# Gate matrix build of a two-layer diffusion trunk: dense selection masks, evacuations on ACT, one gated group in four on GpSimd, more one-hot buffers

## The chip, the cores and the metric

One NeuronCore of a Trainium2 chip runs the whole kernel. The metric is the device time of one execution in microseconds; the median of three runs counts. The engines are TensorE (PE; its weight loads are PEld), VectorE (DVE), ScalarE (ACT), GpSimd (POOL) and SyncE (SP), which only issues DMAs here.

## The reference, cut to what matters

Two layers of a trunk over 640 tokens (128 context, 512 latent). Each layer mixes tokens (gated linear attention, a short convolution, neighbourhood attention) and then retrieves single-neuron experts:

```python
s1 = jnp.einsum('thd,hnd->thn', q[..., :half], k1)      # 8 heads, 128 keys each
s2 = jnp.einsum('thd,hnd->thn', q[..., half:], k2)
v1, i1 = lax.top_k(s1, 16)
v2, i2 = lax.top_k(s2, 16)
cand = v1[..., :, None] + v2[..., None, :]              # 256 candidates a head
cidx = i1[..., :, None] * 128 + i2[..., None, :]
top, pos = lax.top_k(cand, 16)
idx = take_along_axis(cidx, pos); g = softmax(top)      # 128 experts a token
act = gelu(einsum('td,thkd->thk', x, u[idx]))
out = einsum('thk,thkd->td', g * act, v[idx])
```

There are 16384 experts a layer, as 128 rows of 128 columns; expert = 128 * i1 + i2.

## The kernel before

Tokens 0 to 255 take their experts by indirect DMA (`gather`, L736 to L759, issued by POOL). Tokens 256 to 639 are done densely: all 16384 experts are computed in 128 blocks, and each result is multiplied by a gate that is zero for experts that were not chosen. The gates of a token are a 128 x 128 matrix (row of the expert, column of the expert) with 128 nonzero places, one for each choice.

**select(t)** turns the two top-16 lists of 128 tokens into lists of chosen experts, all on DVE but for one exponential. A position in the ordered list of 50 candidates is compared with 16 thresholds (`mask`, L694), the 0/1 mask is multiplied with the differences of the index list (`lookup`, L688), and the 16 products are added by halving (`fold`, L683 and L685). This is done three times: for the first index, for the offset of the row, for the second index. The mask tile is laid out [choice, threshold], with the 16 thresholds last; its two operands are the positions, repeated along the last axis, and the thresholds, repeated along the middle one.

**build(tcn)** makes the gate matrices of 16 tokens. For eight tokens at a time DVE writes two one-hot tiles by comparison with a counter: `ohp` (L776, f32, the expert's row) and `ohq` (L778, bf16, the column). For four tokens at a time ACT multiplies the columns by the gate of each choice, one token an instruction (L782, `qg`), PE multiplies `qg` and `ohp` of each token into PSUM (L785), and the result is evacuated in two parts: the first two groups of rows stay resident in SBUF (`gres`, L787, ACT), the other 14 go to `sg` and from there to DRAM (L795). The spilled part of the first of the four groups of a build is copied by DVE (L791), of the other three by ACT (L793). There are two buffers each of `ohp` and `ohq` and three of `qg`; PSUM has four for these products.

**Order.** After the first top-k stage, peer() runs select(2), then by `ORDER` the builds of tokens 256 to 383 (b2), select(3), b3, select(4), the first top-k of tokens 0 to 127 (l1(0), L610 to L618), b4, select(0). The tile framework lays out each engine's instructions in one fixed order, and independent steps are mixed in it: selects and l1 stand between the builds on DVE. In layer 0, each build also takes a step of the adaLN projection of layer 1 (`next(ada)`, L794: PE, ACT and DVE work and 1 MB of weights). The gate stage, here, is the stretch from the first one-hot tile to the last evacuation: 24 builds a layer.

**After it** come the 128 dense blocks (`dense`): each loads 1 MB, splits it on ACT and DVE (L829, L830), and multiplies on PE; two gathers go with each block.

Of the kernel before, what the change touches and what calls it, by code (L numbers as in the profile page):

```python
# [10 lines left out]
F32 = mybir.dt.float32  # L11
# [4 lines left out]
BF16 = mybir.dt.bfloat16  # L16
F16 = mybir.dt.float16
AF = mybir.ActivationFunctionType
OP = mybir.AluOpType
# [9 lines left out]
PH = 8  # L29
# [29 lines left out]
BSEL = 16  # L59
EVD = 1  # L60
NQG = 3
GLAG = 1
# [3 lines left out]
class Trunk:  # L66
    def __init__(self, ctx, tc, I, O):
# [3 lines left out]
        V, S = self.V, self.S  # L71
        pers = ctx.enter_context(tc.tile_pool(name="pers", bufs=1))
        consts = pers
# [10 lines left out]
        self.ident = const("ident", [128, 128])  # L84
        self.nstep = consts.tile([128, 16], F16, name="nstep16")
        self.thr = consts.tile([128, 2, 16], F16, name="thr16")
        self.iota = consts.tile([128, 128], BF16, name="iota16")
# [4 lines left out]
        with tc.tile_pool(name="init", bufs=1) as ip:  # L92
            for name, shape, dst, dt in (("cT", [128, 8, 2], None, F32), ("lmask", [128, 7, 128], self.lmask, I32),
                                         ("thr", [128, 2, 16], self.thr, F32), ("nstep", [128, 16], self.nstep, F32),
                                         ("iota", [128, 128], self.iota, F32)):
                t = ip.tile(shape, dt, name="i_" + name)
                nc.scalar.dma_start(t, I[name])
                if dst is None:
                    S.activation(self.sc[:, :, 0:2], t, AF.Silu)
                else:  # L100
                    V.tensor_copy(dst, t)
# [463 lines left out]
    def peer(self, l):  # L565
        tc, nc, I = self.tc, self.nc, self.I
        V, S, G, PE = self.V, self.S, self.G, self.PE
# [11 lines left out]
        i12 = [None] * 5  # L579
# [53 lines left out]
        def select(t):  # L633
# [30 lines left out]
            g = gg[t] if t < 2 else ks.tile([128, 128], F32, name="g", tag="g")  # L664
            gv = g.rearrange("p (h k) -> p h k", h=PH)
            V.tensor_tensor(gv, top, top[:, :, 0:1].to_broadcast([128, PH, 16]), op=OP.subtract)
# [3 lines left out]
            V.reciprocal(gz, gz)  # L670
            V.tensor_tensor(gv, gv, gz[:, :, None].to_broadcast([128, PH, 16]), op=OP.mult)
            dl = ks.tile([128, 2, PH, 16], F16, name="dl", tag="dl")
            V.tensor_copy(dl[:, :, :, 0:1], i12[t][:, :, :, 0:1])
            V.tensor_tensor(dl[:, :, :, 1:], i12[t][:, :, :, 1:], i12[t][:, :, :, :15], op=OP.subtract)
            pf = ks.tile([128, 128], F16, name="pf", tag="pf")
            V.tensor_copy(pf, pos.rearrange("p h k -> p (h k)"))
            sh = [128, 128, 16]
            mk = ks.tile(sh, F16, name="mk", tag="mk")
            m2 = ks.tile(sh, F16, name="m2", tag="m2")

            def fold(out, src):
                for w in (8, 4, 2):
                    V.tensor_tensor(m2[:, :, :w], src[:, :, :w], src[:, :, w:2 * w], op=OP.add)  # L683
                    src = m2
                V.tensor_tensor(out, m2[:, :, 0], m2[:, :, 1], op=OP.add)  # L685

            def lookup(out, a):
                V.tensor_tensor(m2.rearrange("p (h k) m -> p h k m", h=PH),  # L688
                                mk.rearrange("p (h k) m -> p h k m", h=PH),
                                dl[:, a, :, None, :].to_broadcast([128, PH, 16, 16]), op=OP.mult)  # L690
                fold(out, m2)

            def mask(a):
                V.tensor_tensor(mk, pf[:, :, None].to_broadcast(sh), self.thr[:, a, None, :].to_broadcast(sh), op=OP.is_ge)  # L694

            ij = ks.tile([128, 3, 128], F16, name="ij", tag="ij")
            mask(0)
            lookup(ij[:, 0], 0)
            V.tensor_tensor(m2, mk, self.nstep[:, None, :].to_broadcast(sh), op=OP.mult)
            fold(ij[:, 2], m2)  # L700
            V.tensor_tensor(pf, pf, ij[:, 2], op=OP.subtract)
            mask(1)
            lookup(ij[:, 1], 1)
            f3 = ks.tile([128, 2, 128], F32, name="f3", tag="f3")
# [65 lines left out]
        def build(tcn):  # L770
            sg = bp.tile([128, NSP, GB, TC], F32, name="sg", tag="sg")
            for t8 in range(0, TC, 8):
                t0 = tcn * TC + t8
                ohp = bp.tile([128, 8, 128], F32, name="ohp", tag="ohp")
                ohq = bp.tile([128, 128, 8], BF16, name="ohq", tag="ohq")
                V.tensor_tensor(ohp, ixT[:, 0, t0:t0 + 8, None].to_broadcast([128, 8, 128]),  # L776
                                self.iota[:, None, :].to_broadcast([128, 8, 128]), op=OP.is_equal)
                V.tensor_tensor(ohq, ixT[:, 1, None, t0:t0 + 8].to_broadcast([128, 128, 8]), iota8, op=OP.is_equal)  # L778
                for t4 in range(0, 8, 4):
                    qg = bp.tile([128, 4, 128], F32, name="qg", tag="qg", bufs=NQG)  # L780
                    for t in range(4):
                        S.activation(qg[:, t, :], ohq[:, :, t4 + t], AF.Copy, scale=gT[:, t0 + t4 + t:t0 + t4 + t + 1])  # L782
                    ps = pss.tile([128, 4, 128], F32, name="ps_g", tag="s")
# [5 lines left out]
                    so, sp = sg[:, :, :, tt:tt + 4].rearrange("p r b t -> p (r b) t"), ps[:, :, NR * GB:].rearrange("p t b -> p b t")  # L789
                    if (tt // 4) % 4 < EVD:  # L790
                        V.tensor_copy(so, sp)  # L791
                    else:
                        S.activation(so, sp, AF.Copy)  # L793
            next(ada, None)  # L794
# [206 lines left out]
```

## Time and profile before

| what | value |
|---|---|
| median of three runs (lowest, highest) | 4094.76 us (4085.15, 4112.63) |
| the profiled execution | 4098.88 us, its span 4097.1 us |
| busy in the span | PE 92%, DVE 81%, ACT 42%, POOL 18% |
| mean granted clock of PE | 0.951 of 2.4 GHz |
| bytes over the DMA queues | 1011.79 MB, mean 247 GB/s |

A profile describes one execution. "Busy" is time in which an engine has an instruction under way; PE's ends are modelled. Instructions of one engine overlap a little in the profile, so the distance between two starts is a better price than the duration of one. A line such as L785 is a line of the kernel.

### The profile page before, as it was taken

What the parts mean: (1) busy time and instruction counts of PE and PEld (TensorE: products, weight loads), DVE (VectorE), ACT (ScalarE), POOL (GpSimd) and SP (SyncE); (2) the same over time, 40 slices, a digit from 0 to 9 for tenths busy, and PEclk for the clock granted to TensorE, in tenths of its full rate; (3) what the DMA queues carried; (4) which work ended last, traced back from release to release, by engine and by line L of the source; (5) the groups of instructions that cost most, each with busy time, mean ns of one, the idle gap of its engine ahead of it and who ended that gap; (6) DMA issues with size and microseconds to landing.
All of it is one profiled execution on the core that took longest, in us unless ns stands there. A gap on an engine that the chain in (4) does not pass through costs nothing.

```text
span 4097.1 us, 52986 instructions
## 1 busy us (share of the span) xinstructions
PE 3752.5 (92%) x19892; PEld 3210.2 (78%) x19892; DVE 3324.4 (81%) x6613; ACT 1701.8 (42%) x3269; POOL 755.8 (18%) x532
## 2 busy tenths in 40 slices
PE   7999996888999999999989999867799999999998
PEld 5897875557888888888879988745688888888886
DVE  3863478778999999999968533988899999999997
ACT  4423334883333333333354242378633333333333
POOL 0000000003333333333300000000133333333331
PEclk8999997878999999999999999978799999999999
DMA  5114142648999999999911121022699999999995
GB/s 178 33 61 139 65 144 80 190 133 345 381 378 388 382 382 383 391 379 386 364 53 34 61 65 52 32 72 90 226 366 377 382 383 385 379 386 382 380 379 211
DMA packets 263089, 1011.79 MB, mean 247 GB/s; under 512 B 21872, under 2 KB 110320, under 8 KB 164272
## 3 DMA queue, kind: packets, MB, share of 16 engines
q0 software_dynamic: 73728, 536.90, 34.0%
q1 hardware_dynamic: 171392, 425.43, 27.8%
q10 hardware_dynamic: 17712, 46.07, 2.9%
q8 instruction: 157, 2.57, 0.2%
q14 instruction: 100, 0.82, 0.1%
HBM read 960.49 MB, written 47.84 MB: 246 GB/s over the span
## 4 chain that ended last, share of the span: by engine, by line
issue 34%; PE 34%; POOL 11%; DVE 8%; ACT 8%; DMA 5%; POOLq 0%; ACTq 0%; DVEq 0%; SPq 0%
PE ps_pj L225 13%; POOL uv L745 11%; DMA uv<-uv,gidx 4%; ACT qg L782 4%; PE ps_g L785 4%; PE acc L868 3%; PE ps_lv L353 2%; PE ps_ada L150 2%; PE npo L519 1%; ACT sg L793 1%; PE ps_ms L167 1%; PE ps_s L498 1%; PE ps_a L852 1%; PE ps_a L851 1%; PE ps_a L850 1%
## 5 line engine op out<-in xcount | busy, mean ns | idle before, releaser
L745 POOL DMA_INDIRECT uv<-uv,gidx x512 | 748.5, 1462 | 3272.0 <-DVE gacc L757 1354.2
L850 PE MATMUL ps_a<-hd,uhi 128*128 128x384 f32 x2048 | 693.9, 339 | 33.8 <-ACT uhi L829 33.8
L852 PE MATMUL ps_a<-hd,ulo 128*128 128x384 f32 x2048 | 693.3, 339 | 10.0 <-DVE ulo L830 10.0
L851 PE MATMUL ps_a<-hd,uhi 128*128 128x384 f32 x2048 | 692.0, 338 | 0.0
L748 DVE SCALAR_TENSOR_TENSOR uv<-uv,ht 128x1024 f32<-128x1024 f32 x512 | 622.5, 1219 | 84.0 <-DMA uv<-uv,gidx 83.0
L757 DVE SCALAR_TENSOR_TENSOR gacc<-uv,gw,gacc 128x1024 f32<-128x1024 f32 x508 | 652.1, 1284 | 15.5
L868 PE MATMUL acc<-vhi,whi 128*128 128x512 f32 x1536 | 504.3, 410 | 33.9 <-ACT whi L860 33.3
L868 PE MATMUL acc<-vhi,wlo 128*128 128x512 f32 x1536 | 483.0, 396 | 15.8 <-DVE wlo L861 15.7
L829 ACT ACTIVATE vhi<-raw 128x1024 fp32r<-128x1024 f32 x256 | 272.2, 1063 | 537.6 <-PE acc L868 523.1
L868 PE MATMUL acc<-vlo,whi 128*128 128x512 f32 x1536 | 477.5, 392 | 0.0
L850 PEld LDWEIGHTS ps_a<-hd,uhi 128*128 128x128 f32 x2048 | 387.9, 189 | 46.5 <-ACT uhi L829 36.2
L785 PE MATMUL ps_g<-ohp,qg 128*128 128x128 f32 x1536 | 333.2, 359 | 83.5 <-ACT qg L782 82.2
L785 PEld LDWEIGHTS ps_g<-ohp,qg 128*128 128x128 f32 x1536 | 261.4, 235 | 184.4 <-ACT qg L782 142.6
L852 PEld LDWEIGHTS ps_a<-hd,ulo 128*128 128x128 f32 x2048 | 387.4, 189 | 16.6 <-DVE ulo L830 14.6
L851 PEld LDWEIGHTS ps_a<-hd,uhi 128*128 128x128 f32 x2048 | 387.9, 189 | 10.2
L868 PEld LDWEIGHTS acc<-vhi,whi 128*128 128x128 f32 x1536 | 270.0, 188 | 128.2 <-ACT whi L860 81.2
L782 ACT ACTIVATE qg<-ohq,gT 128x128 f32<-128x128 bf16 x768 | 339.6, 526 | 65.7 <-DVE ohq L778 65.7
L868 PEld LDWEIGHTS acc<-vhi,wlo 128*128 128x128 f32 x1536 | 282.8, 188 | 92.6 <-DVE wlo L861 34.4
L868 PEld LDWEIGHTS acc<-vlo,whi 128*128 128x128 f32 x1536 | 289.0, 188 | 65.0
L830 DVE TENSOR_TENSOR vlo<-raw,vhi 128x1024 fp32r<-128x1024 f32 x256 | 311.8, 1218 | 16.0 <-ACT vhi L829 15.9
L830 DVE TENSOR_TENSOR ulo<-raw,uhi 128x1024 fp32r<-128x1024 f32 x256 | 312.2, 1220 | 2.1 <-ACT uhi L829 2.0
L750 ACT ACTIVATE gw<-dots 128x2 f32<-128x2 f32 x256 | 52.0, 203 | 610.0 <-DVE uv L748 610.0
(242 smaller groups left out, 6085.6 us busy)
## 6 DMA issues: line engine op xcount, KB each, us to landing
raw<-dn SPq DMA_DIRECT2D x256, 1024.0 KB
wada<-w_ada SPq DMA_DIRECT2D x48, 1024.0 KB
gsp<-sg SPq DMA_DIRECT2D x48, 896.0 KB
gres<-gsp ACTq DMA_DIRECT2D x112, 384.0 KB
wraw<-w_in SPq DMA_DIRECT2D x56, 512.0 KB
wraw<-w_out SPq DMA_DIRECT2D x16, 512.0 KB
wraw<-wq SPq DMA_DIRECT2D x16, 512.0 KB
uv<-uv,gidx POOLq DMA_INDIRECT x512
```

Of the source, the lines that this page charges most:

```text
L225: self.PE.matmul(ps[j][:, :n], w[:, k, :], x[:, k, :], start=(k == 0 and i == 0), stop=(k == 7 and i == 2))
L745: G.indirect_dma_start(out=b, out_offset=None, in_=I["uv"], in_offset=bass.IndirectOffsetOnAxis(ap=gidx[t][:, s:s + 1], axis=0))
L748: V.scalar_tensor_tensor(b[:, :D], b[:, :D], 1.0, ht[t], op0=OP.mult, op1=OP.mult, accum_out=dots[:, s:s + 1])
L757: V.scalar_tensor_tensor(acc_, b[:, D:], w[:, s:s + 1], acc_, op0=OP.mult, op1=OP.add)
L782: S.activation(qg[:, t, :], ohq[:, :, t4 + t], AF.Copy, scale=gT[:, t0 + t4 + t:t0 + t4 + t + 1])
L785: PE.matmul(ps[:, t, :], qg[:, t, :], ohp[:, t4 + t, :], start=True, stop=True)
L829: S.activation(hi, raw, AF.Copy)
L830: V.tensor_tensor(lo, raw, hi.bitcast(F32), op=OP.subtract)
L850: PE.matmul(ps, uhi[:, ks], hd[0][:, k, :], start=(k == 0), stop=False)
L851: PE.matmul(ps, uhi[:, ks], hd[1][:, k, :], start=False, stop=False)
L852: PE.matmul(ps, ulo[:, ks], hd[0][:, k, :], start=False, stop=(k == 7))
L868: PE.matmul(acc[:, t, j, :], a[:, ts], x[:, j * 512:(j + 1) * 512], start=(b == 0 and i == 0), stop=(b == 127 and i == len(parts) - 1))
```

## The change

Three things.

1. In `select` the mask, the differences, the positions and the constants are laid out with the head (8 of them) as the last axis, so that both operands of a mask have a dense last axis, and the folds run over the outer axis. The choices of a token are numbered by (choice, head) and no longer by (head, choice), in the gates too. The exponentials are written to the first 16 columns of the candidate tile.
2. In `build`, the gated rows of the last of four groups are made by one GpSimd product over four tokens; the other three stay on ACT. ACT evacuates the spilled part of all four groups.
3. Buffers: `qg` 5 for 3, `ohp` 3 for 2, `ohq` 4 for 2.

```diff
-EVD = 1
-NQG = 3
+NQG = 5
+QGP = (3,)
@@ constants
-        self.nstep = consts.tile([128, 16], F16, name="nstep16")
-        self.thr = consts.tile([128, 2, 16], F16, name="thr16")
+        self.nstep = consts.tile([128, 16, PH], F16, name="nstep16")
+        self.thr = consts.tile([128, 2, 16, PH], F16, name="thr16")
+                elif name in ("thr", "nstep"):
+                    V.tensor_copy(dst, t[..., None].to_broadcast(shape + [PH]))
@@ select
-            gv = g.rearrange("p (h k) -> p h k", h=PH)
+            gv = cand[:, :, :16]
...
-            V.tensor_tensor(gv, gv, gz[:, :, None].to_broadcast([128, PH, 16]), op=OP.mult)
-            dl = ks.tile([128, 2, PH, 16], F16, name="dl", tag="dl")
+            V.tensor_tensor(g.rearrange("p (k h) -> p h k", h=PH), gv, gz[:, :, None].to_broadcast([128, PH, 16]), op=OP.mult)
+            dl = ks.tile([128, 2, 16, PH], F16, name="dl", tag="dl")
...
-            pf = ks.tile([128, 128], F16, name="pf", tag="pf")
-            V.tensor_copy(pf, pos.rearrange("p h k -> p (h k)"))
-            sh = [128, 128, 16]
+            pf = ks.tile([128, 16, PH], F16, name="pf", tag="pf")
+            V.tensor_copy(pf, pos.rearrange("p h k -> p k h"))
+            sh = [128, 16, 16, PH]
...
-                    V.tensor_tensor(m2[:, :, :w], src[:, :, :w], src[:, :, w:2 * w], op=OP.add)
+                    V.tensor_tensor(m2[:, :w], src[:, :w], src[:, w:2 * w], op=OP.add)
                     src = m2
-                V.tensor_tensor(out, m2[:, :, 0], m2[:, :, 1], op=OP.add)
+                V.tensor_tensor(out.rearrange("p (k h) -> p k h", h=PH), m2[:, 0], m2[:, 1], op=OP.add)
+            def per(x):
+                return x[:, :, None, :].to_broadcast(sh)
...
-                V.tensor_tensor(mk, pf[:, :, None].to_broadcast(sh), self.thr[:, a, None, :].to_broadcast(sh), op=OP.is_ge)
+                V.tensor_tensor(mk, pf[:, None].to_broadcast(sh), per(self.thr[:, a]), op=OP.is_ge)
@@ build
-                ohp = bp.tile([128, 8, 128], F32, name="ohp", tag="ohp")
-                ohq = bp.tile([128, 128, 8], BF16, name="ohq", tag="ohq")
+                ohp = bp.tile([128, 8, 128], F32, name="ohp", tag="ohp", bufs=3)
+                ohq = bp.tile([128, 128, 8], BF16, name="ohq", tag="ohq", bufs=4)
...
-                    for t in range(4):
-                        S.activation(qg[:, t, :], ohq[:, :, t4 + t], AF.Copy, scale=gT[:, t0 + t4 + t:t0 + t4 + t + 1])
+                    if (t8 + t4) // 4 in QGP:
+                        G.tensor_tensor(qg.rearrange("p t q -> p q t"), ohq[:, :, t4:t4 + 4],
+                                        gT[:, None, t0 + t4:t0 + t4 + 4].to_broadcast([128, 128, 4]), op=OP.mult)
+                    else:
+                        for t in range(4):
+                            S.activation(qg[:, t, :], ohq[:, :, t4 + t], AF.Copy, scale=gT[:, t0 + t4 + t:t0 + t4 + t + 1])
...
-                    if (tt // 4) % 4 < EVD:
-                        V.tensor_copy(so, sp)
-                    else:
-                        S.activation(so, sp, AF.Copy)
+                    S.activation(so, sp, AF.Copy)
```

## Rows read from the trace of the kernel before

**Rows 1.** Windows, dense stretches: busy (count) of PE, PEld, DVE, ACT, POOL; PEclk, DMA, GB/s.

```profile
1000.00:1950.00 950.00, 922.83 (x4563) 812.23 (x4562) 896.02 (x1208) 340.46 (x542) 321.06 (x219) 1.00 0.97 383
3000.00:3950.00 950.00, 919.40 (x4530) 805.84 (x4528) 890.04 (x1200) 338.54 (x540) 317.66 (x217) 1.00 0.97 381
```

**Rows 2.** Windows: before layer 1's gate stage, the stage itself, layer 0's gate stage.

```profile
2648.00:2689.30 41.30, 9.04 (x36) 6.25 (x34) 41.30 (x244) 2.08 (x3) 0.00 (x0) 0.62 0.00 1
...
2689.30:2915.30 226.00, 177.27 (x782) 136.26 (x782) 187.59 (x560) 205.34 (x555) 2.09 (x3) 0.81 0.30 95
675.00:921.00 246.00, 211.50 (x1016) 143.46 (x1017) 186.51 (x545) 210.54 (x559) 0.20 (x1) 0.83 0.53 163
```

**Rows 3.** Chain that ended last, shares by line: layer 1's gate stage, then layer 0's.

```profile
by line: ACT qg L782 45.7%; PE ps_g L785 24.2%; ACT sg L793 12.5%; ACT gres L787 5.0%; issue 1.9%; DVE i L614 1.4%; DVE i L618 1.4%; DVE ohp L776 1.2%; POOL uv L745 1.1%; DVE v L616 1.0%; DVE s L612 0.9%; DVE ohq L778 0.9%; DVE v L610 0.7%;
by line: PE ps_g L785 37.6%; ACT qg L782 21.4%; PE ps_ada L150 18.2%; ACT sg L793 7.4%; ACT gres L787 3.3%; DMA uv<-uv,gidx 2.7%; PE ps_at L157 2.5%; DVE ohp L776 1.4%; issue 1.1%; DVE i L618 0.9%; DVE ohq L778 0.7%; DVE v L616 0.6%; DVE i 
```

**Rows 4.** Waits, layer 1's gate stage: waiter <- releaser: us in total, times, longest.

```profile
ACT qg L782 <- DVE ohq L778: 33.0, 3, 19.5
...
DVE ohq L778 <- ACT qg L782: 15.2, 29, 1.9
DVE sg L791 <- ACT gres L787: 13.6, 22, 1.1
DVE ohp L776 <- PE ps_g L785: 8.4, 17, 1.5
```

**Rows 5.** Timeline at the seam to b4: start, length, engine, line [idle before it].

```profile
2829.74 0.42 DVE L715 CAST ixT<-pt 128x256 bf16<-128x256 f32 x1 [0.88 <-PE pt L713]
...
2844.46 3.83 ACT L782 ACTIVATE qg<-ohq,gT 128x128 f32<-128x128 bf16 x9 [12.91 <-DVE ohq L778]
```

**Rows 6.** Timeline of ACT in layer 1's gate stage, steady state.

```profile
2766.43 0.54 ACT L793 ACTIVATE sg<-ps_g 128x448 f32<-128x448 f32 x1
2766.86 1.76 ACT L782 ACTIVATE qg<-ohq,gT 128x128 f32<-128x128 bf16 x4
2768.51 0.21 ACT L787 ACTIVATE gres<-ps_g 128x64 f32<-128x64 f32 x1
2768.61 0.54 ACT L793 ACTIVATE sg<-ps_g 128x448 f32<-128x448 f32 x1
```

**Rows 7.** DVE by line and shape (L791: layer 1's stage): count, busy us, mean ns, idle.

```profile
L778 DVE TENSOR_TENSOR ohq<-ixT,iota 128x1024 bf16<-128x1024 bf16 x96 | 66.1, 688 | 31.3 <-ACT qg L782 31.2
L694 DVE TENSOR_TENSOR mk<-pf,thr 128x2048 f16<-128x2048 f16 x20 | 45.7, 2285 | 0.1
L688 DVE TENSOR_TENSOR m<-mk,dl 128x2048 f16<-128x2048 f16 x20 | 24.4, 1219 | 0.0
L685 DVE TENSOR_TENSOR ij<-m 128x128 f16<-128x128 f16 x30 | 11.7, 390 | 0.1
L683 DVE TENSOR_TENSOR m<-m 128x256 f16<-128x256 f16 x30 | 11.7, 389 | 0.1
L701 DVE TENSOR_TENSOR pf<-pf,ij 128x128 f16<-128x128 f16 x10 | 2.2, 219 | 0.1
...
L791 DVE COPY sg<-ps_g 128x448 f32<-128x448 f32 x24 | 15.0, 624 | 13.6 <-ACT gres L787 13.6
```

**Rows 8.** POOL's memsets; then gather issues and L830: ns min/median/max, first and last start.

```profile
L281 POOL MEMSET qz<- 64x640 f32 x8 | 5.0, 627 | 14.6 <-DVE gacc L757 14.1 <-POOLq L992 0.3
L282 POOL MEMSET st<- 64x256 f32 x8 | 2.4, 304 | 0.0
...
L745 POOL DMA_INDIRECT uv<-uv,gidx x512: 933/1674/3284, 920.8 to 4041.7; - x171
...
L830 DVE TENSOR_TENSOR ulo<-raw,uhi x256: 1210/1220/1226, 933.5 to 4045.1; 128x1024 fp32r<-128x1024 f32 x128
L830 DVE TENSOR_TENSOR vlo<-raw,vhi x256: 1211/1218/1227, 941.6 to 4048.9; 128x1024 fp32r<-128x1024 f32 x128
```

**Rows 9.** Windows, L785 alone: PE and PEld busy (count), PEclk, DMA share, GB/s.

```profile
2724.00:2731.00 7.00, 5.59 (x27) 3.86 (x26) 1.00 0.42 131
2804.50:2812.50 8.00, 7.39 (x31) 6.64 (x30) 0.50 0.36 115
```

More of the change, by code (lines that the diff above doesn't have):

```diff
@@ L670, in select @@
             V.reciprocal(gz, gz)
-            V.tensor_tensor(gv, gv, gz[:, :, None].to_broadcast([128, PH, 16]), op=OP.mult)
-            dl = ks.tile([128, 2, PH, 16], F16, name="dl", tag="dl")
-            V.tensor_copy(dl[:, :, :, 0:1], i12[t][:, :, :, 0:1])
-            V.tensor_tensor(dl[:, :, :, 1:], i12[t][:, :, :, 1:], i12[t][:, :, :, :15], op=OP.subtract)
-            pf = ks.tile([128, 128], F16, name="pf", tag="pf")
-            V.tensor_copy(pf, pos.rearrange("p h k -> p (h k)"))
-            sh = [128, 128, 16]
+            V.tensor_tensor(g.rearrange("p (k h) -> p h k", h=PH), gv, gz[:, :, None].to_broadcast([128, PH, 16]), op=OP.mult)
+            dl = ks.tile([128, 2, 16, PH], F16, name="dl", tag="dl")
+            ix = i12[t].rearrange("p a h m -> p a m h")
+            V.tensor_copy(dl[:, :, 0:1, :], ix[:, :, 0:1, :])
+            V.tensor_tensor(dl[:, :, 1:, :], ix[:, :, 1:, :], ix[:, :, :15, :], op=OP.subtract)
+            pf = ks.tile([128, 16, PH], F16, name="pf", tag="pf")
+            V.tensor_copy(pf, pos.rearrange("p h k -> p k h"))
+            sh = [128, 16, 16, PH]
             mk = ks.tile(sh, F16, name="mk", tag="mk")
@@ L682, in fold, with lookup @@
                 for w in (8, 4, 2):
-                    V.tensor_tensor(m2[:, :, :w], src[:, :, :w], src[:, :, w:2 * w], op=OP.add)
+                    V.tensor_tensor(m2[:, :w], src[:, :w], src[:, w:2 * w], op=OP.add)
                     src = m2
-                V.tensor_tensor(out, m2[:, :, 0], m2[:, :, 1], op=OP.add)
[L687 to L690, printed above, removed]
+                V.tensor_tensor(out.rearrange("p (k h) -> p k h", h=PH), m2[:, 0], m2[:, 1], op=OP.add)
+            def per(x):
+                return x[:, :, None, :].to_broadcast(sh)
+            def lookup(out, x):
+                V.tensor_tensor(m2, mk, per(x), op=OP.mult)
                 fold(out, m2)
             def mask(a):
-                V.tensor_tensor(mk, pf[:, :, None].to_broadcast(sh), self.thr[:, a, None, :].to_broadcast(sh), op=OP.is_ge)
+                V.tensor_tensor(mk, pf[:, None].to_broadcast(sh), per(self.thr[:, a]), op=OP.is_ge)
             ij = ks.tile([128, 3, 128], F16, name="ij", tag="ij")
             mask(0)
[L698 to L701, printed above, removed]
+            lookup(ij[:, 0], dl[:, 0])
+            lookup(ij[:, 2], self.nstep)
+            V.tensor_tensor(pf, pf, ij[:, 2].rearrange("p (k h) -> p k h", h=PH), op=OP.subtract)
             mask(1)
-            lookup(ij[:, 1], 1)
+            lookup(ij[:, 1], dl[:, 1])
             f3 = ks.tile([128, 2, 128], F32, name="f3", tag="f3")
```

## The prediction

> **What bounds the kernel now.** I read the windows first, then the chain of waits inside the stretch that the change touches, then who waited there, then single durations. The two dense stretches, where all 128 expert blocks of a layer run, hold the DMA engines at 0.97 of their time and PE at 0.97 busy with the full clock granted [rows 1]. The change removes no byte and no matmul there, so nothing can be won in them. The work that is edited lies in the gate stage of each layer: 24 builds, 226.0 us in layer 1 and 246.0 us in layer 0, with the DMA engines at 0.30 and 0.53, plus the stretch before it in which select(2) runs alone and DVE is busy for 41.30 of 41.30 us [rows 2]. Whatever comes off these comes off the end one for one, since the dense stretch starts when the last build is out.
>
> In layer 1's gate stage ACT is busy 205.3 us, DVE 187.6, PE 177.3 [rows 2]. The chain agrees: 45.7 + 12.5 + 5.0 = 63.2% of it is ACT (gating the one-hot rows, then the two evacuations) and 24.2% PE. In layer 0 the adaLN matmuls of the next layer are mixed in, and the chain turns: PE has 37.6 + 18.2 + 2.5 = 58.3%, ACT 21.4 + 7.4 + 3.3 = 32.1% [rows 3]. So a gift to ACT is worth about half as much in layer 0. ACT's own waits are one start-up wait of 19.5 us, which began before the stage, and one of 12.9 us at the seam to the last eight builds [rows 4, 5]: there DVE finishes the index lists at 2829.74 but works through the rest of l1(0) before the next one-hot tile, and ACT starts again only at 2844.46.
>
> **ACT's part.** In steady state a gating quartet takes ACT from 2766.86 to 2768.51, 1.65 us; the resident part 0.10; the spilled part from 2766.43 to 2766.86, 0.43 [rows 6]. Per build the change takes one quartet of four from ACT and gives it the one spilled part that DVE copied: 1.65 - 0.43 = 1.22 us less. Over 24 builds that is 29.3 us, so ACT goes from 205.3 to 176.0 in layer 1.
>
> **DVE's part, without POOL.** The 24 copies of L791 leave: 15.0 us, and with them 13.6 us of waiting for ACT [rows 4, 7]. In every select, two masks of 2048 elements take 2.285 us, while the product on the same 2048 half-precision elements, whose last axis is dense, takes 1.219 [rows 7]. After the edit the masks' last axis is eight dense elements in both operands. That eight are enough I read from L778: a comparison too, last axis eight, 1024 elements in 0.688. So 2 x (2.285 - 1.219) = 2.13 us. The rows at 2048 (1.219) and 128 (0.219) elements make 0.52 ns an element and 0.15 fixed, which gives 0.29 for the dense fold of 256 in place of 0.389, and 0.219 for the last fold in place of 0.390 [rows 7]; three folds a select save 3 x 0.10 + 3 x 0.17 = 0.81. Together 2.9 us a select; the bound below is nothing (masks that stay at 2.285). Select(2) stands bare ahead of each stage: 2 x 2.9 = 5.9 us straight off the end. Three more selects run inside each stage: 8.8 us of DVE time. DVE in layer 1 goes to 187.6 - 15.0 - 8.8 = 163.8.
>
> **The product on POOL.** POOL is idle in the stage (2.1 us busy) [rows 2], so nothing stands ahead of the product in its queue. Behind it, PE's four matmuls of that group wait for it, then every later matmul in PE's order, then ACT's evacuations of that group. No row shows an elementwise operation of POOL. Its memsets take 0.627 us for 640 elements and 0.304 for 256 [rows 8]: 0.84 ns an element and 0.09 fixed. One pass over 512 elements would be 0.52 us, the floor. Two reads and one write, one after another, make 1.38. The same engine's gather issue takes 0.93 us at best and 1.67 in the median, when DVE is busy beside it, 1.8 times as much [rows 8]; that factor gives 2.5, and the longest gather, 3.28, is my upper end. I take 1.9, between 1.38 and 2.5. Even 3.28 is below the 7.3 us that ACT will need for a build (176.0 / 24), so POOL itself is not the bound.
>
> What it takes from DVE is the open price. Below: nothing, because L830, which reads two SBUF tensors, takes 1210 to 1227 ns in 512 instances, most of them in a stretch where POOL issues its gathers [rows 8]. Above: the whole product, since a gather issue hardly reads SBUF and the product reads two operands. I take 1.2 us, some two thirds of 1.9, because a part of DVE's work in the stage (the top-k searches) has one operand. The Trainium skill speaks against the change here: "SBUF — State Buffer", section "Who interferes with whom", says that a DVE instruction with two SBUF inputs and a GpSimd instruction that reads SBUF exclude each other for the whole instruction. By that rule the price is the full length of the product, which is the second rival below; the rows of L830 neither show nor exclude it. The Trainium skill's "GPSIMD Engine Reference", section 3.1, gives 4497 ns for a two-input operation on 2048 elements, which no run here shows; an estimate from that page is 1.1 us for 512, DVE's price at the same two thirds 0.7, and the sum 12 us shorter a layer.
>
> **Parts at nothing.** The one-hot and gated tiles take more buffers; that costs no instruction, and it takes away some of DVE's 15.2 and 8.4 us of waiting for ACT and PE [rows 4]. The permuted gate weights, index differences and positions have as many instructions as before. The exponentials now lie in the candidate tile, so the next select's candidates wait for one more small product. The two longer constant copies stand at the kernel's start beside the first loads; bare they would be under 1 us. Select(1) runs in the dense stretch, behind DMA [rows 1]. With POOL as idle as it is, the last product is out before the first gather may go.
>
> **PE's clock.** In the stretch 2724 to 2731 the full clock is granted and PE, paced by ACT, is busy 5.59 of 7.00 us; in 2804.5 to 2812.5 it is 1.2 GHz and PE is busy 7.39 of 8.00 [rows 9]. So a build at 1.2 GHz has little room left below today's pace; this caps the gain wherever the clock stays low, and I count it in layer 0.
>
> **The sum.** Layer 1: DVE 163.8 + 24 x 1.2 = 192.6, above ACT's 176.0. DVE sat idle for 226.0 - 187.6 = 38.4 us; 13.6 go with the copies and the deeper buffers take part of the rest, so I leave 12. That makes 204.6, 21 us less. Layer 0: ACT's relief by its share of the chain, 29.3 x 32.1 / 63.2 = 15 us. Select(2): 5.9. In all 42.2 us. The profiled execution took 4098.9 us (span 4097.1); 4098.9 - 42.2 = 4056.7. The median of the runs, 4094.8, is 4.1 lower, so I forecast 4053 for the median.
>
> **The rivals.**
> - DVE loses nothing to POOL and ACT stays the bound. For it: L830's even durations. Layer 1 gains the full 29.3, layer 0 perhaps 22, plus 5.9: 57 us, 4037. If the wait of 12.9 us at the seam goes too, in both layers, 4012.
> - The product shuts DVE out for its whole length of 1.9 us, or the masks stay at 2.285. For it: DVE will be close behind ACT. DVE is then 163.8 + 45.6 + 12 = 221, a gain of 5 a layer and 5.9: 4079. Without the masks' gain (5.9 in all and 8.8 in each layer lost) the forecast would be 4076. By the exclusion rule of the Trainium skill, named above, the first half of this is the case.
> - Slower: the product is long under DVE's traffic and shuts DVE out. The point that decides is a loss of (226.0 - 163.8 - 12) / 24 = 2.1 us a build. At 3.28, DVE has 163.8 + 78.7 + 12 = 254.5, 28.5 us more in each layer; less 5.9 that is 51 us, 4146. For it: four-element runs and a strided output, on an engine that no row shows at such work. Against it: it needs both the long product and the full exclusion.
>
> **How the numbers follow.** Measurement of this kernel tells about 1% from no change, so faster is below 4054, slower above 4136. Forecast (4040 to 4066): 0.38. First rival (4010 to 4040): 0.25. Second (4066 to 4100): 0.26. Slower side: 0.11, of which 0.09 beyond 1%. Faster is the first rival and two thirds of the forecast's band, 0.50; same 0.41; slower 0.09. The range 4015 to 4092 leaves out the slower side and the outermost of the first two. The forecast's own range is 4040 to 4066.
>
> **What would show it.** Right: L694 near 1.22 us; ACT in layer 1's stage near 176 us; the stage near 205; a POOL product near 1.9 us; L776 and L778 lengthened or held up beside it by about 1.2 us a build; the stretch before the stage 3 us shorter. Wrong: L776 even at 1.22 with no idle time (first rival); products above 2.5 us with DVE near 100% busy (second, third); a seam wait that grows as ACT runs ahead of DVE.

## The result and the profile after

The changed kernel takes 4027.59 us in the median (4024.19 to 4033.49), the kernel before, run beside it, 4101.16 us (4085.15 to 4112.63). The ratio is 0.9826, with a 95% interval from 0.9807 to 0.9844: 74 us less by the two medians, 71 by the ratio, where 42 were forecast. The profiled execution after took 4028.24 us (span 4026.5), against a span of 4097.1 before, so the two profiles differ by 70.6 us.

Where these 70.6 us went, read from the starts of four lines in both traces (first one-hot tile; last gate matmul; first transposition of the second gathered tile of tokens, some 8 us before that of the dense blocks' output; end):

| stretch | before | after | difference |
|---|---|---|---|
| up to layer 0's first one-hot tile | 675.0 | 675.3 | +0.3 |
| layer 0's gate stage | 247.9 | 199.6 | -48.3 |
| layer 0's dense stretch | 1136.9 | 1154.8 | +17.9 |
| up to layer 1's first one-hot tile | 629.6 | 622.9 | -6.7 |
| layer 1's gate stage | 225.0 | 191.6 | -33.4 |
| layer 1's dense stretch | 1143.7 | 1143.0 | -0.7 |
| the rest | 39.0 | 39.3 | +0.3 |

The gate stages gave 81.7 us, and the dense stretches, which the change does not touch, took back 17.2. These are two single executions; how far they repeat is said further down. Below, the "stage" is always the stretch of this table. The windows shown run 0.2 to 1.3 us past it, so where a microsecond matters, busy times are taken over the stage itself (DVE 175.5 and 176.2 us in the changed kernel, layer 0 and layer 1).

Windows of the changed kernel: layer 0's gate stage, layer 1's, and the stretch before layer 1's in which DVE runs select(2); columns as in [rows 1]. They answer to [rows 2].

```profile
675.30:876.20 200.90, 169.76 (x1022) 122.98 (x1022) 176.69 (x503) 180.81 (x493) 41.19 (x25) 0.92 0.68 201
2652.60:2845.40 192.80, 143.18 (x782) 113.87 (x782) 177.40 (x501) 174.00 (x483) 39.90 (x25) 0.91 0.40 113
2629.60:2652.60 23.00, 0.90 (x3) 0.50 (x3) 23.00 (x139) 0.31 (x1) 0.00 (x0) 0.50 0.00 0
```

In layer 1 ACT is down from 205.34 to 174.00 us. DVE is down only from 187.59 to 177.40, so the two are now level, and the stage is 15 us longer than DVE's work. PE does the same matmuls in 143.18 us instead of 177.27, at a granted clock of 0.91 instead of 0.81. POOL, which had been empty, is busy for 39.90 us.

The chain that ended last, shares by line, in layer 1's stage and then in layer 0's (they answer to [rows 3]):

```profile
by line: ACT qg L789 42.8%; ACT sg L797 17.7%; PE ps_g L792 10.4%; ACT gres L794 6.6%; DVE ohp L779 5.5%; DMA uv<-uv,gidx 4.9%; DVE ohq L781 2.3%; issue 2.2%; DVE i L620 1.7%; DVE s L614 1.2%; DVE mk L698 1.2%; DVE i L616 1.1%; DVE v L618 0
by line: PE ps_g L792 28.9%; ACT qg L789 21.5%; ACT sg L797 10.6%; PE ps_ada L152 8.4%; DVE ohp L779 4.3%; PE ps_at L159 4.1%; DMA uv<-uv,gidx 3.8%; issue 3.5%; ACT gres L794 3.5%; DVE ohq L781 3.0%; POOL qg L785 2.4%; ACT arow L156 2.1%; P
```

In layer 1 PE's part falls from 24.2% to 10.4%, ACT keeps 67.1% of the chain (63.2% before), and DVE's one-hot tiles rise from 2.1% to 7.8%. In layer 0 the adaLN matmuls fall from 18.2% to 8.4%: a line that the diff does not name.

DVE's groups of the changed kernel by line and shape: count, busy us, mean ns, idle before them. The first is the f32 one-hot tile (L776 before), then the masks, and two of the folds; they answer to [rows 7].

```profile
L779 DVE TENSOR_TENSOR ohp<-ixT,iota 128x1024 f32<-128x1024 bf16 x96 | 138.0, 1438 | 12.3 <-PE ps_g L792 11.9
L698 DVE TENSOR_TENSOR mk<-pf,thr 128x2048 f16<-128x2048 f16 x20 | 24.3, 1213 | 0.2
L686 DVE TENSOR_TENSOR m<-m 128x256 f16<-128x256 f16 x30 | 9.0, 301 | 0.3
L688 DVE TENSOR_TENSOR ij<-m 128x128 f16<-128x128 f16 x30 | 7.3, 244 | 0.2
```

Waits in layer 1's stage after, waiter <- releaser: us in total, times, longest (answering to [rows 4]).

```profile
ACT qg L789 <- DVE ohq L781: 29.8, 3, 16.7
DVE ohp L779 <- PE ps_g L792: 6.0, 9, 1.6
DVE ohq L781 <- ACT qg L789: 4.0, 11, 0.4
```

DVE's waits for ACT, 15.2 and 13.6 us before, are 4.0. The wait at the seam to b4 is still there, 10.41 us where [rows 5] had 12.91:

```profile
2785.90 3.86 ACT L789 ACTIVATE qg<-ohq,gT 128x128 f32<-128x128 bf16 x9 [10.41 <-DVE ohq L781]
```

### The profile page after: what moved, and what is told of

Read it like the earlier page. It is cut to its first block, busy times and chain, and to the rows that moved or that the text cites. A ratio compares the mean times of both kernels' runs of the same rounds, so it can differ in the third digit from the quotient of the medians.

```text
span 4026.5 us, 52976 instructions
## 1 busy us (share of the span) xinstructions
PE 3683.3 (91%) x19892; PEld 3168.4 (79%) x19892; DVE 3296.0 (82%) x6565; ACT 1638.6 (41%) x3125; POOL 833.9 (21%) x580
## 4 chain that ended last, share of the span: by engine, by line
PE 35%; issue 29%; DVE 11%; POOL 9%; DMA 8%; ACT 8%; POOLq 0%; ACTq 0%; DVEq 0%
PE ps_pj L227 13%; POOL uv L748 9%; DMA uv<-uv,gidx 7%; PE acc L872 5%; ACT qg L789 3%; PE ps_lv L355 2%; PE ps_g L792 2%; PE ps_a L856 1%; PE ps_ada L152 1%; PE ps_a L855 1%; PE ps_a L854 1%; ACT sg L797 1%; PE npo L521 1%; PE ps_ms L169 1%; DVE gacc L760 1%
## 5 line engine op out<-in xcount | busy, mean ns | idle before, releaser
L785 POOL TENSOR_TENSOR qg<-ohq,gT 128x512 f32<-128x512 bf16 x48 | 80.8, 1688 | 1590.2 <-PE ps_g L792 1501.6
L792 PE MATMUL ps_g<-ohp,qg 128*128 128x128 f32 x1536 | 270.5, 318 | 74.9 <-ACT qg L789 73.6
L792 PEld LDWEIGHTS ps_g<-ohp,qg 128*128 128x128 f32 x1536 | 219.9, 208 | 139.7 <-ACT qg L789 111.5
## 6 DMA issues: line engine op xcount, KB each, us to landing
gres<-gsp ACTq DMA_DIRECT2D x112, 384.0 KB, 12.6
```

Source lines behind the costliest of these rows:

```text
L792: PE.matmul(ps[:, t, :], qg[:, t, :], ohp[:, t4 + t, :], start=True, stop=True)
```

## The experiments

The theory (A): ACT set the pace of the gate stage, and the POOL product took it off; what the stage keeps is DVE's work. Its rivals: (B) the deeper buffers did it; (C) PE's clock did it: more of the full clock was granted, and the shorter gate matmuls are the gain; (D) the dense masks did it, since DVE fed everyone. Later came (F): layer 0's surplus over layer 1 comes from where the tile framework put the adaLN matmuls. No run changes what is computed.

**Buffers alone**, the kernel before with the change's buffers:

```diff
-NQG = 3
+NQG = 5
-                ohp = bp.tile([128, 8, 128], F32, name="ohp", tag="ohp")
-                ohq = bp.tile([128, 128, 8], BF16, name="ohq", tag="ohq")
+                ohp = bp.tile([128, 8, 128], F32, name="ohp", tag="ohp", bufs=3)
+                ohq = bp.tile([128, 128, 8], BF16, name="ohq", tag="ohq", bufs=4)
```

> The kernel before with the buffers of the change alone (gated rows 5, row one-hots 3, column one-hots 4). Theory A (ACT's 1.22 us a build is the gain, and PE's clock follows from it): ACT keeps all its work, so the gate stages stay near 248 us (layer 0) and 225 us (layer 1) from the first one-hot tile to the last gate matmul; at most 5 us off each, the end within 10 us of before. Rival B (the deeper buffers are the gain, because DVE and PE no longer wait for a free tile): layer 0 near 215, layer 1 near 205, the end 40 us or more earlier.

Measured: 4124.51 us, ratio 1.0068 (1.0047 to 1.0089): 25 us more, where theory A allowed 10 either way. The stages are 247.0 and 223.6 us, as before. The loss lies in the dense stretches, 1160.0 and 1163.2 us in the profiled execution, which was the run's longest (4141.27 us; the other three took 4121 to 4125). B falls.

**The changed kernel without the product**, so that ACT gates all groups and still evacuates all:

```diff
-QGP = (3,)
+QGP = ()
```

> The changed kernel with no product on POOL: ACT gates all four groups and evacuates all four. ACT then has 24 x 0.43 us more than before the change, 215 us a stage. Theory A: layer 1's gate stage is 225 to 240 us, layer 0's 240 to 260, and the end is within 20 us of the kernel before on either side (select's 5.4 us stay won). Rival B (buffers) or a rival in which the masks and DVE's lost copies do it: layer 1 at 210 or less, layer 0 at 225 or less, the end 30 us or more before the kernel before. The one-hot comparisons should be 1.22 us with no lengthening, since nothing on POOL reads SBUF.

Measured: 4116.62 us, ratio 1.0049 (1.0032 to 1.0065); stages 253.7 and 227.1 us. Windows of this run, layer 0's stage and layer 1's:

```profile
672.90:927.00 254.10, 219.06 (x1022) 147.60 (x1022) 163.76 (x499) 223.00 (x588) 1.68 (x2) 0.81 0.52 159
2701.70:2929.10 227.40, 179.44 (x782) 138.87 (x782) 161.34 (x486) 215.57 (x577) 1.59 (x2) 0.80 0.34 94
```

ACT, with the copies that DVE gave up, has 215.57 us and the stage is 12 us longer than that; DVE has 161.34 and is idle for nearly a third of the stage. With the product the same kernel's stages are 54 and 36 us shorter. The product is what the change lives on: A holds, for the product in company with the change's other parts. This run also gives DVE's work without a product beside it, 163.76 us in layer 0 and 161.34 in layer 1 (163.5 and 161.1 over the stages themselves).

**Each gate matmul issued twice**, in the kernel before (PE overwrites the same result):

```diff
                         PE.matmul(ps[:, t, :], qg[:, t, :], ohp[:, t4 + t, :], start=True, stop=True)
+                        PE.matmul(ps[:, t, :], qg[:, t, :], ohp[:, t4 + t, :], start=True, stop=True)
```

> The kernel before with each gate matmul issued twice into the same place (the second result, the same, stays). PE has twice the gate work and no engine has less. Theory A in its plain form (PE's clock is no limit): the gate stages get longer or stay, layer 0 above 250 us. Rival C (PE's clock at 1.2 GHz in a part of the stage is a limit by itself; PE kept busy is granted the full clock and is then faster by more than the added work): granted clock in layer 0's stage rises from 0.83 to 0.95 or more, the adaLN matmuls fall from 45 to 32 us, and layer 0's stage falls by 10 us or more though PE does more; layer 1's stays near 225.

Measured: 4108.45 us, ratio 1.0016 (0.9995 to 1.0037). Windows, layer 0's stage and layer 1's:

```profile
676.80:941.70 264.90, 234.63 (x1790) 213.26 (x1790) 204.44 (x619) 210.04 (x565) 3.89 (x4) 0.89 0.53 168
2697.70:2922.00 224.30, 189.26 (x1550) 183.24 (x1550) 187.15 (x584) 201.99 (x551) 4.77 (x4) 0.94 0.34 108
```

In layer 1 twice the gate matmuls fit into the same 224 us, PE is busy 12 us longer and the granted clock rose from 0.81 to 0.94. So PE had room there and its clock was no limit: C falls for layer 1. In layer 0 PE has 234.63 us of work and the stage is 17 us longer, at a clock of 0.89 where C wanted 0.95, so this run does not say what the clock alone is worth in layer 0. That stays open.

**The dense masks alone**: the constants and select of the diff in the kernel before, with its builds and buffers:

```diff
-            sh = [128, 128, 16]
+            sh = [128, 16, 16, PH]
...
```

> The kernel before with the dense masks alone (the build unchanged). Expected by theory A: select(2) 25.2 to 22.5 us in both layers; three more selects inside each stage free 8 us of DVE, which is not the bound there; the seam wait of ACT before b4 (10 and 12.9 us) gets some 3 us shorter; in all 6 to 14 us off the end. A rival in which DVE is the true limit of the stage: 20 us or more off.

Measured: 4092.97 us, ratio 0.9989 (0.9977 to 1.0000). Windows, layer 0's stage and layer 1's:

```profile
673.70:909.30 235.60, 203.58 (x1022) 134.93 (x1022) 176.25 (x522) 210.70 (x563) 3.89 (x4) 0.91 0.56 175
2676.40:2895.40 219.00, 174.50 (x782) 131.40 (x782) 175.78 (x512) 203.38 (x553) 3.13 (x4) 0.86 0.36 100
```

Select(2) takes 22.4 us instead of 25.1, as forecast, and DVE has 12 us less in the stage. In this profile the stages are shorter by 12.5 and 6.4 us, while ACT has its old 203 us in layer 1. The profiled execution was the run's shortest, 4077.7 us, and the median keeps only 0.1%. D explains a small part by itself. The change without the masks was not run; since DVE's work is what layer 1's stage follows after the change (below), the masks may be worth more there.

**The changed kernel with the old buffers** (`NQG = 3`, two `ohp` and two `ohq`):

> The changed kernel with the old buffers (gated rows 3, row one-hots 2, column one-hots 2). Theory A (ACT's relief): the gate stages stay near those of the change, 200 and 192 us, at most 8 us longer each. Rival B' (the buffers are needed, because DVE and POOL must run ahead of ACT): 215 or more in layer 0 and 207 or more in layer 1, the end 30 us later than the changed kernel. Rival D (the deeper buffers alone made the dense stretches 23 us longer in their run, so they cost there): dense stretches back from 1151 and 1141 to some 1132 to 1140, which offsets the stages, the end within 10 us of the changed kernel or earlier.

Measured: 4026.72 us, ratio 0.9824 (0.9808 to 0.9840); stages 199.7 and 192.6 us. Windows, layer 0's stage and layer 1's:

```profile
674.50:874.60 200.10, 170.56 (x1022) 122.32 (x1022) 173.11 (x544) 179.81 (x491) 34.64 (x27) 0.93 0.69 202
2641.70:2834.70 193.00, 143.15 (x782) 116.41 (x782) 170.86 (x522) 173.99 (x481) 32.65 (x26) 0.89 0.39 110
```

The third part of the change contributes nothing. DVE is even less busy, 173.11 and 170.86 us instead of 176.69 and 177.40, although more of select's instructions fall into the stage (544 and 522 DVE instructions in the windows instead of 503 and 501). Why, the single durations show. First the changed kernel's comparison of the f32 one-hot tile, its POOL product and the comparison of the bf16 tile (ns min/median/max, first and last start):

```profile
L779 DVE TENSOR_TENSOR ohp<-ixT,iota x96: 1201/1220/2065, 675.3 to 2833.8; 128x1024 f32<-128x1024 bf16 x96
L785 POOL TENSOR_TENSOR qg<-ohq,gT x48: 1077/1249/4880, 679.1 to 2835.9; 128x512 f32<-128x512 bf16 x48
L781 DVE TENSOR_TENSOR ohq<-ixT,iota x96: 660/684/1530, 676.4 to 2828.4; 128x1024 bf16<-128x1024 bf16 x96
```

The same three lines with the old buffers:

```profile
L779 DVE TENSOR_TENSOR ohp<-ixT,iota x96: 1199/1218/1231, 674.5 to 2827.5; 128x1024 f32<-128x1024 bf16 x96
L785 POOL TENSOR_TENSOR qg<-ohq,gT x48: 1088/1111/2047, 679.2 to 2830.2; 128x512 f32<-128x512 bf16 x48
L781 DVE TENSOR_TENSOR ohq<-ixT,iota x96: 667/692/1408, 675.7 to 2826.9; 128x1024 bf16<-128x1024 bf16 x96
```

And the f32 comparison without a product:

```profile
L779 DVE TENSOR_TENSOR ohp<-ixT,iota x96: 1209/1224/1227, 672.9 to 2916.2; 128x1024 f32<-128x1024 bf16 x96
```

With two buffers DVE begins the next f32 tile later, when the product is out: one of 96 runs beside a product, and none is lengthened. With three, 44 run beside a product, and 28 are lengthened, to as much as 2065 ns. The collision is not gone with the old buffers: 11 bf16 comparisons take over 0.72 us (5 with the new ones), and steps of select are lengthened too. Each DVE instruction of a stage, held against the mean of the same instruction in the run without a product, gives a sum (worked out from the durations): 6.8 us in layer 0 and 6.6 in layer 1 with the old buffers, 12.6 and 13.6 with the new ones. The deeper buffers move DVE's work into the collision, and what they save in waiting they lose there.

**The product issued twice**, in the changed kernel:

```diff
-                        G.tensor_tensor(qg.rearrange("p t q -> p q t"), ohq[:, :, t4:t4 + 4],
-                                        gT[:, None, t0 + t4:t0 + t4 + 4].to_broadcast([128, 128, 4]), op=OP.mult)
+                        for _ in range(2):
+                            G.tensor_tensor(qg.rearrange("p t q -> p q t"), ohq[:, :, t4:t4 + 4],
+                                            gT[:, None, t0 + t4:t0 + t4 + 4].to_broadcast([128, 128, 4]), op=OP.mult)
```

> The changed kernel with every POOL product issued twice into the same place. ACT, PE and the buffers keep their work; POOL's doubles. With the products DVE is busy 176 us a stage, without them 162 to 164: 12 to 15 us for 24 products, 0.5 to 0.6 us each. Theory E (a product and a DVE instruction with two SBUF inputs shut each other out): DVE busy goes to 188 to 192 us, the lengthened comparisons become about twice as many, and layer 1's stage goes from 192 to 198 or more. Rival (the price is paid once a build, by a late start, whatever POOL's work): DVE stays at 176 to 180 and the stages within 4 us.

Measured: 4040.15 us, ratio 0.9847 (0.9827 to 0.9868); stages 201.2 and 198.1 us. Window of layer 1's stage:

```profile
2658.20:2856.50 198.30, 148.18 (x782) 120.55 (x782) 185.87 (x487) 173.59 (x481) 81.90 (x48) 0.87 0.38 107
```

Over the stages themselves DVE has 185.7 us against 176.2 in layer 1 and 186.8 against 175.5 in layer 0: 24 more products cost it 9.5 and 11.3 us, 0.39 and 0.47 us each. Layer 1's stage grows by 6.5 us, layer 0's by 1.6. ACT's work is unchanged. Of the f32 comparisons 33 are lengthened instead of 28, of the bf16 ones 19 instead of 5. The sum of the lengthenings, which does not depend on how much of select falls into the stage, gives one price throughout: 0.53 and 0.57 us for each of the 24 products of the changed kernel (layer 0, layer 1), 0.52 and 0.50 for each of the 48 here, and 0.28 with the old buffers. This is the price measured by itself: well below the length of a product, and above nothing.

**Two groups of four on POOL**:

```diff
-QGP = (3,)
+QGP = (1, 3)
```

> The changed kernel with two of four groups made on POOL (second and fourth). ACT loses another 24 x 1.65 = 40 us a stage (173 to 133 in layer 1); DVE is lengthened by another 12 to 15 us (176 to 190). If ACT is still what sets the stage, layer 1 falls from 192 to 160 to 175. If DVE has come level with ACT (theory A with E), layer 1 stays at 190 to 203 us and layer 0 at 195 to 212: nothing won, up to 20 us lost at the end.

Measured: 4027.94 us, ratio 0.9828 (0.9806 to 0.9851). Windows, layer 0's stage and layer 1's:

```profile
672.80:867.80 195.00, 147.64 (x1022) 120.50 (x1022) 175.35 (x479) 141.74 (x394) 78.40 (x48) 0.85 0.68 206
2650.40:2837.20 186.80, 126.19 (x782) 107.44 (x782) 173.86 (x472) 135.79 (x386) 82.95 (x48) 0.83 0.41 114
```

Another 38 us come off ACT and the stages lose 5 us each; the total does not move. DVE, which I had expected at 190, is at 173.86: 13 us under the stage's length, about as in the changed kernel (15). It is not that the products became free: the 48 lengthen DVE's instructions by 21.8 and 21.0 us (0.45 and 0.44 each). But about 9 us of select's steps now come after the stage's end (472 DVE instructions in layer 1's window, 501 in the changed kernel's). Layer 0's stage is shorter than the changed kernel's though more of its gate matmuls ran at 1.2 GHz, 131 of 768 instead of 91.

**One evacuation of four back on DVE**, in the changed kernel:

```diff
-                    S.activation(so, sp, AF.Copy)
+                    if (tt // 4) % 4 < 1:
+                        V.tensor_copy(so, sp)
+                    else:
+                        S.activation(so, sp, AF.Copy)
```

> The changed kernel with the first spilled part of each build copied by DVE again. ACT loses 24 x 0.43 = 10 us (173 to 163 in layer 1), DVE gains 15 (176 to 191) and waits for ACT's resident part before each copy. If ACT sets the stage: 10 us a stage less. If both are level: DVE becomes the longest and the stages grow by 5 to 15 us each.

Measured: 4040.77 us, ratio 0.9857 (0.9834 to 0.9879). Window of layer 1's stage:

```profile
2649.40:2845.00 195.60, 142.59 (x782) 112.57 (x782) 181.63 (x495) 162.22 (x457) 32.94 (x24) 0.88 0.38 109
```

Over the stage itself ACT has 162.0 us to do against 172.8 in the changed kernel, DVE 181.3 against 176.2, and the stages are 3.4 and 3.7 us longer. So after the change DVE's work is what layer 1's stage follows, although the chain gave ACT two thirds of it. Its length is DVE's busy time plus 12 to 15 us in the changed kernel and in these three runs (192.8, 198.3, 186.8, 195.6 against 177.4, 185.9, 173.9, 181.6). Only with the old buffers is it 22, beside an ACT of 173.99. In layer 0, where PE has the adaLN matmuls besides, the stage is 14 to 24 us longer than DVE's busy time in the same four runs, so DVE alone does not set it there.

**The adaLN matmuls kept together**, in the kernel before. Why this was asked: of the four matmuls of an adaLN step, each on its own 32 columns of PE, the kernel before issues one, then gate matmuls, then the other three. PE's timeline there:

```profile
703.40 1.04 PE L150 MATMUL ps_ada<-wada,sc 128*32 128x512 f32 x2
704.38 0.94 PE L785 MATMUL ps_g<-ohp,qg 128*128 128x128 f32 x6
705.24 1.06 PE L150 MATMUL ps_ada<-wada,sc 128*32 128x512 f32 x6
```

In the changed kernel some steps run whole (x8: four matmuls, two records each), the others stay split:

```profile
684.59 1.06 PE L152 MATMUL ps_ada<-wada,sc 128*32 128x512 f32 x8
...
686.23 1.04 PE L152 MATMUL ps_ada<-wada,sc 128*32 128x512 f32 x2
...
688.75 1.06 PE L152 MATMUL ps_ada<-wada,sc 128*32 128x512 f32 x6
```

Four together take as long as one alone. The edit raises their priority in the framework's order, so that they stay together:

```diff
-                for i in range(4):
-                    PE.matmul(ps[32 * i:32 * i + 32, :], self.sc[:, 4 * h + i, :], w[:, i, :], start=not h, stop=bool(h))
+                with self.tc.high_priority():
+                    for i in range(4):
+                        PE.matmul(ps[32 * i:32 * i + 32, :], self.sc[:, 4 * h + i, :], w[:, i, :], start=not h, stop=bool(h))
```

> The kernel before; only the four adaLN matmuls of a step (four column groups of PE, able to run side by side) are given priority so that they stand together in PE's fixed order. Before, one stood alone and three followed after gate matmuls; in the changed kernel half the steps have all four together. Theory F (this reshuffle is why layer 0 gained 48 us and layer 1 only 33): adaLN matmuls busy in layer 0's stage 47.6 to 21 to 30 us, layer 0's stage 248 to 225 to 238 us, layer 1's 225 as before, the end 10 to 20 us earlier. Rival (the adaLN work was covered by ACT's, and layer 0 gained through PE's clock): layer 0's stage within 5 us of 248.

Measured: 4085.62 us, ratio 0.9972 (0.9956 to 0.9989). Layer 0's stage is 232.6 us, 15.3 less than in the kernel before; layer 1's, which has no adaLN step, is 223.6 (1.4 less). PE's groups of these matmuls (count, busy us, mean ns of one, idle) in the kernel before, in the changed kernel, in this run and in the run with two groups on POOL:

```profile
L150 PE MATMUL ps_ada<-wada,sc 128*32 128x512 f32 x160 | 47.6, 627 | 0.0
```

```profile
L152 PE MATMUL ps_ada<-wada,sc 128*32 128x512 f32 x160 | 31.7, 605 | 0.0
```

```profile
L151 PE MATMUL ps_ada<-wada,sc 128*32 128x512 f32 x160 | 23.0, 699 | 0.0
```

```profile
L152 PE MATMUL ps_ada<-wada,sc 128*32 128x512 f32 x160 | 22.2, 627 | 11.0 <-DMA wada<-w_ada 10.4 <-ACT sg L797 0.6
```

F holds. 24.6 us of PE time less are worth 15.3 us of layer 0. The change had won 15.9 of the 24.6 by accident; in proportion that would be 10 of its 48.3 us, an estimate. With two groups on POOL the matmuls stand together without any priority (22.2 us), so the 5 us that layer 0 lost in that run cannot be put down to the second group alone.

**The same in the changed kernel**, and **in the changed kernel with two groups on POOL** (the edit above, and `QGP = (1, 3)` besides):

> The changed kernel with the same priority for the adaLN matmuls. Theory F: adaLN busy 31.7 to some 21 us, layer 0's stage 200 to 188 to 196, layer 1's 192 as before, the end 4 to 12 us before the changed kernel. Rival: layer 0's stage stays at 200.

> The changed kernel with that priority and two of four groups on POOL (which alone gave stages of 195 and 187 us). If the two add up: layer 0's stage 183 to 192, layer 1's 187, the end 10 us or more before the changed kernel, unless the dense stretches, which lay between 1126 and 1163 us in the runs so far, take it back.

Measured: 4024.84 us, ratio 0.9816 (0.9802 to 0.9829), with stages of 195.6 and about 192 us; and 4023.01 us, ratio 0.9816 (0.9799 to 0.9834), with 192.5 and 185.5 us. Both are the shortest seen, but their intervals overlap with that of the changed kernel, so neither can be called better than it. Layer 0 loses 4 us where the kernel before lost 15: half of the steps were whole already, and other work comes next. With two groups on POOL all but one were whole already, and the priority takes 2 us off layer 0's stage.

**The changed kernel once more**, unedited:

> The changed kernel again, unedited, to see what one profiled execution is worth. If the dense stretch is set by the order of its instructions: layer 0 at 1151 and layer 1 at 1141 us, within 4 us, as in its first profile. If it varies from one execution to the next: differences of 8 us or more in at least one. The gate stages should return within 2 us (199.9 and 191.9).

Measured: 4033.06 us, ratio 0.9828 (0.9812 to 0.9844). Its stages are 199.6 and 190.9 us, within a microsecond of the first profile. Its dense stretches are 1153.3 and 1151.4 us, where the first had 1154.8 and 1143.0, and the 17 us that they took back are 24 in this execution. So the gate stage repeats to a microsecond and the dense stretch to eight or so.

**What the dense stretch does.** In the runs with the old buffers it took 1126.5 to 1148.9 us (kernel before, buffers restored, masks alone, matmul twice, adaLN together; ten stretches, mean 1142). In those with the deeper ones it was 1143.0 to 1163.2 (nine runs, 18 stretches, mean 1152). Windows of 950 us inside layer 0's dense stretch, the changed kernel and then the buffers alone:

```profile
890.00:1840.00 950.00, 910.38 (x4445) 797.55 (x4443) 877.77 (x1193) 335.41 (x532) 307.72 (x211) 0.99 0.95 374
```

```profile
1000.00:1950.00 950.00, 912.11 (x4480) 798.62 (x4481) 884.08 (x1194) 333.87 (x533) 320.34 (x214) 1.00 0.95 375
```

[rows 1] had DMA at 0.97 and 383 GB/s: the same traffic at a 2% lower rate. What costs this was not found, and with the old buffers in the changed kernel (1144.7 and 1146.6 us, where 1132 to 1140 were expected) the median is the same within its interval, so it is not shown that the buffers are the cause.

## Why the prediction was right, and where not

The forecast was 4053 us (4015 to 4092). The direction and the range held; the measured 4027.6 lies in the band that the prediction gave to its first rival. That rival's reason, that DVE loses nothing to POOL, is not what happened. Luck had a part in the range: the dense stretches took back 17 us that no term had foreseen, and without them the time would have been near 4010, below the range's 4015.

- **Select.** Right. 2.9 us a select were forecast and 2.7 came; the masks are at 1213 ns (1.22), the folds at 301 and 244 (0.29 and 0.219). In front of layer 0 nothing of it shows (+0.3): there select(2) takes 23.1 us instead of 25.7, from its first candidate to the first one-hot tile, but begins 3.0 us later. In front of layer 1 there are 6.7 us less, of which select(2) is 2.7; the second execution of the changed kernel had 4.2 less.
- **ACT's part.** Right: 176.0 us forecast, 174.00 measured.
- **DVE without POOL.** Right: 163.8 us forecast, 161.34 and 163.76 in the run without a product.
- **The product's length.** 1.9 us forecast. The mean is 1688 ns, but the median is 1249 and the shortest 1077 (median 1111 with the old buffers): the taken value was too long for the product itself, and the rest is waiting for DVE. The Trainium skill's "GPSIMD Engine Reference", section 3.1, led to an estimate of 1.1 us; the trace agrees with it, by its shortest products.
- **What it takes from DVE.** The mis-sized term. I took 1.2 us a product, 28.8 a layer. Measured: DVE's instructions are lengthened by 12.6 and 13.6 us, 0.53 and 0.57 us a product; 0.28 with the old buffers, and 0.44 to 0.52 where there were 48 products. L830's even durations beside the gathers [rows 8], which spoke for nothing, did not carry over to an operation that reads two tiles. Two thirds of 1.9 was too much because the product is shorter, and because the waiting falls on both sides: every one of the 48 products overlaps a DVE instruction with two inputs, but the products wait too, 0.6 us each in the mean (1688 less 1077 ns). Of the 96 f32 comparisons, the 52 that overlap no product have a mean of 1217 ns, the 44 that do 1698 (worked out from the starts and durations of both lines). With the 177.4 measured, the forecast's own form, DVE plus 12, would have been 189 for layer 1; it is 191.6.
- **Layer 0 at half price.** Failed, and it is the largest miss: 15 us forecast, 48.3 measured. ACT's share of the chain (32%) was read as the share of the gift that the layer would keep. But the layer has two engines in turn on its chain, and both got shorter. PE's busy time over the stage fell from 213.1 to 169.5 us. 15.9 of that is the order of the adaLN matmuls, which nothing in the diff announces. The gate matmuls have 27.9 us less: 237 of the 768 ran at 1.2 GHz before (440 ns in the mean) and 91 after, and at 2.4 GHz they took 307 and 296 ns, so that by an estimate some 20 of the 27.9 come with the clock.
- **"This caps the gain wherever the clock stays low."** Failed. The clock did not stay low: 0.83 to 0.92 in layer 0, 0.81 to 0.91 in layer 1. Of layer 1's 768 gate matmuls 253 ran at 1.2 GHz before and 93 after. The row I read (1.2 GHz, PE 7.39 of 8.00 us busy [rows 9]) was a state that came with the old pace of feeding and not a property of the stage: with twice the matmuls and the same 224 us the clock was 0.94. Whether the rise itself bought time in layer 0 is open; in layer 1 the doubled matmuls show that PE was no limit before it.
- **Parts at nothing.** The buffers: right, nothing. "Nothing can be won" in the dense stretches: right, but I had not asked what could be lost, and 17 us were.
- **The seam.** Left in the sum as idle time, and it stayed: 10.41 us.

Terms put together: layer 1 gave 33.4 for 21, layer 0 48.3 for 15, the stretches ahead of them 6.4 for 5.9, and the dense stretches took back 17.2 for 0. The 46 us too few and the 17 too many make the miss of 28.

A slower kernel, for which the prediction wanted 2.1 us a product, was far off at 0.53 to 0.57.

## What to carry to other kernels

When the engine that sets a stage is relieved, work out where the next one stands from its own busy time in that stage plus its unavoidable idle time; do not scale the relief by shares of a chain, since the chain is made anew. In a stage that another engine paces, do not take a low granted clock of PE for a cap: here twice the matmuls left the stage at 224 us and the clock rose from 0.81 to 0.94. After an edit, look at the order of the instructions that it did not touch: here four matmuls kept together were worth 15 us of a stage, and stretches that nobody had edited became 17 us longer for a reason that was not found.

## What the runs showed of the hardware

DVE's comparison of two SBUF tiles and POOL's product over two SBUF tiles do hold each other up. A pair from the changed kernel's timeline (start, length, engine, line), the comparison begun 0.23 us after the product, and below it the next one with no product beside it:

```profile
2698.18 1.25 POOL L785 TENSOR_TENSOR qg<-ohq,gT 128x512 f32<-128x512 bf16 x1 [5.90 <-PE ps_g L792]
...
2698.41 2.06 DVE L779 TENSOR_TENSOR ohp<-ixT,iota 128x1024 f32<-128x1024 bf16 x1
...
2703.32 1.22 DVE L779 TENSOR_TENSOR ohp<-ixT,iota 128x1024 f32<-128x1024 bf16 x1
```

The comparison takes 0.84 us longer, close to what was left of the product (1.02). In the other direction products of 1.1 us are stretched to as much as 4.88. That one began 0.23 us into a comparison, and DVE's next four, one right behind the other, ran undisturbed before it ended (the row merges it with the product behind it):

```profile
816.48 1.22 DVE L779 TENSOR_TENSOR ohp<-ixT,iota 128x1024 f32<-128x1024 bf16 x1
816.71 5.89 POOL L785 TENSOR_TENSOR qg<-ohq,gT 128x512 f32<-128x512 bf16 x2 [17.03 <-DVE ohq L781]
817.62 1.89 DVE L781 TENSOR_TENSOR ohq<-ixT,iota 128x1024 bf16<-128x1024 bf16 x3
819.42 1.22 DVE L779 TENSOR_TENSOR ohp<-ixT,iota 128x1024 f32<-128x1024 bf16 x1
```

The Trainium skill's "SBUF — State Buffer", section "Who interferes with whom", says that such a pair shuts each other out for the whole instruction; the trace agrees in kind. The price in the kernel is smaller than a product's length: about half a microsecond of DVE's time for each product of 1.1 us, and 0.28 with the old buffers; the rest of the waiting is the product's own.

Four f32 matmuls of 512 columns, each on its own 32 columns of PE, take 1.06 us when they are issued back to back, as long as one alone (1.04). Split into one and three they cost 2.10.
